# A conditioned hybrid decoder layer: the Pool-weight fold in four groups over blocks, the gate in the output-side stage, and own rings for two sets of small and large tiles

## The chip, the cores and the metric

The kernel runs on one core of one Trainium2 chip. Its time is the device time of one launch in microseconds (us), given as the median of several runs. One execution of the kernel before was also recorded by the hardware profiler; all rows that are quoted come from that execution. The engines are PE (matrix products; its weight loads are listed as PEld), DVE (vector), ACT (scalar functions), POOL and SP. SP issues nearly all transfers between main memory and the on-chip memory, in order.

## The reference

The layer works on x of 4096 tokens by 1024 channels, in float32, with one conditioning vector c.

```
shift, scale, gate = split(SiLU(c) @ w_ada + b_ada)          # 3 x 1024
h   = LN(x) * (1 + scale) + shift
u_a | z_a | glu_b | z_b = split(h @ w_in + b_in)             # 512, 512, 1024, 512
y_a = SiLU(z_a) * ls * (GroupLinear(CausalMultiPool(u_a) - u_a) + b_pool)
v   = glu_b[:, :512] * sigmoid(glu_b[:, 512:])
y_b = SiLU(z_b) * (SiLU(LN(DWConv31(v)) * g + b) @ w_pw + b_pw)
y   = concat(y_a, y_b) @ w_out + b_out
out = LN(2 ** 0.25 * x + gate * y) * ln_post_g + ln_post_b
```

CausalMultiPool is a trailing mean over 2, 4, 8 or 16 tokens, one width for each group of 128 channels. Pooling acts along the tokens and GroupLinear along the channels, so the weights of GroupLinear can be multiplied into the u_a part of w_in ahead of time. The kernel does this, and the document calls it the fold.

## The kernel before

**Tiling.** Tokens are cut in eight blocks (sb) of T = 512, each of TT = 4 row tiles of 128 tokens. Channels are cut in KT = 8 slices of 128 (k). Every float32 matrix is split in a high part in PE's reduced float32 type and the low rest (`split`, L194): ACT makes the high part with a copy, DVE subtracts it from the source. `mm3` (L336) makes one product of three matmuls: high times high (L337), high times low (L338), low times high (L339). A chunk is 128 output channels for one block: 8 slices of 3 matmuls of 512 columns, 24 in all.

**Stages.** Stage 1 (L461) goes over the eight blocks. In each it makes ten chunks: eight for the gated unit of mixer B (chunk pairs 8+m and 12+m, m = 0 to 3) and two of z_b (`z_half`, L454). Stage 2 (L512) reads the normalised x again from main memory (xD, written in stage 1) and makes ten more chunks a block: z_a, u_a and the rest of z_b. Between matmuls DVE runs the depthwise convolution of finished blocks (`conv`, L558), which takes most of its time, and `conv_ln` (L588) its LayerNorm. Stage 3 (L761) makes the second product of mixer B and the output product, with the last two blocks' convolutions beside it.

**The first block** is made in another way than the others. Its four x tiles are loaded by row (`load_x`, L258) and normalised (L375 to L377). `mod_block` (L173) works out shift and scale for one or two slices of channels: eight DVE steps multiply the w_ada tiles by SiLU(c) and add them up in `macc` (L179, L181), and PE sums `macc` over the partitions by a matmul with one column of ones (L186). `turn_x` (L313) transposes x on PE, and `mod_turned` (L319) applies scale and shift and makes the high and the low part (L321, L323, L324). The rows of w_in for the eight gated chunks (`load_row`, L389) are 128 by 1024 and are split by `split_cols` (L402), 768 and then 256 columns. Block 0 then runs six of its eight gated chunks k by k over six banks (L420), and the last pair, m = 3, in the loop at L473.

**The other blocks** of stage 1 are prepared one block ahead. `row_stats` (L278) loads four row tiles, takes their mean and variance by two ACT passes (`col_stats`, L263: L265 and L267) with small DVE steps and a power on POOL (L269), turns the results to rows (`to_rows`, L271), writes them out and reads them back to all partitions (`xbc`, L286). `norm_T` (L289) loads transposed x and applies the statistics on DVE (L292, L294); `mod_xT` (L298) adds the shift and makes the high part on ACT (L303) and the low part on DVE (L304), and stores both to xD (L306).

**The work that the change moves.** Behind block 0, `fold_u` (L350) is called four times, once for each group g: it loads a slice wT of the transposed w_in (L352), makes 16 matmuls of 128 columns (L358), two copies on ACT, a store, and one small matmul for the bias. Behind block 1, `mod_gate` (L140) adds up the gate from eight w_ada tiles on DVE, and four matmuls spread it over the partitions (L495). The 16 stores of block 0's xT (L439) stand behind the first block's products, with a wait for the last step of `mod_block`.

**Buffers.** A tag names a ring of buffers; a tile waits until the ring's oldest tile has been read. The tag `tm` (5 buffers) holds x tiles, `xbc` and `norm_T`'s tiles; `wraw` (2) holds raw weights; `gate` and `gbo` (1 each) hold weight rows, then the gate and the output bias; `ca` (6) holds w_ada tiles and then convolution tiles; `sm` (4) and `rows8` (2) are shared by the statistics of x and of the convolution.

**Order.** The program is written stage by stage, and a scheduler writes out the order on each engine from a simulated timeline; each engine then works strictly in that order. A few orders are given by hand with `after` (L84).

Of the kernel before, what the change touches and what calls it, by code (L numbers as in the profile page):

```python
# [9 lines left out]
F32 = mybir.dt.float32  # L10
# [7 lines left out]
P = 128  # L18
# [15 lines left out]
EARLY = 2  # L34
PERSB = (1, 1, 1, 1, 1, 1, 0, 0)
# [4 lines left out]
def tile_layer(ctx, tc, x, x_t, w_in_t, c, w_ada, b_ada, w_in, b_in, w_pool, b_pool, ls_pool, w_dw, b_dw,  # L40
# [132 lines left out]
    def mod_block(b, k0, nk, wts):  # L173
# [3 lines left out]
        for kt in range(KT):  # L177
# [6 lines left out]
        for i in range(2):  # L184
            for j in range(nk):
                nc.tensor.matmul(ps[:, nk * i + j : nk * i + j + 1], acc[:, 1 - i, j * P : (j + 1) * P],  # L186
                                 ones[:, 0:1], start=True, stop=True)
# [33 lines left out]
    def stats_dve(src, n, pre, i):  # L221
        nh = n // 512
        bs = st.tile([P, nh, 6], F32, tag=f"{pre}bs", bufs=4, name=f"{pre}bs{i}")
# [34 lines left out]
    def load_x(i):  # L258
        xt = ph.tile([P, D], F32, tag="tm", bufs=5, name=f"x{i}")
        nc.sync.dma_start(xt, tok(xv, i))  # L260
# [27 lines left out]

    def norm_T(sb, bc, k):  # L289
        z = ph.tile([P, 2, T], F32, tag="tm", bufs=5, name=f"xk{sb}_{k}")  # L290
        nc.sync.dma_start(z, x_t[k * P : (k + 2) * P, sb * T : (sb + 1) * T].rearrange("(k p) s -> p k s", p=P))
# [58 lines left out]
    def fold_u(g, wpl):  # L350
        wT = wraw(f"wT{g}")
        nc.sync.dma_start(wT, w_in_t[g * P : (g + 1) * P, :])  # L352
        wf = wraw(f"wf{g}")
        for hb in range(2):
            pb = s2_bank(f"fv{g}_{hb}")
# [6 lines left out]
        pb = s2_bank(f"bu{g}")  # L362
# [39 lines left out]
    def split_cols(k, m0, m1):  # L402
        split(*(t.rearrange("p (h c) -> p h c", h=2)[:, :, m0 * P : m1 * P] for t in (*Wg[k], rows[k])))
# [31 lines left out]
    gate_bc = cst.tile([P, D], F32, tag="gate", name="gate_bc")  # L435
    gbo = cst.tile([P, D], F32, tag="gbo", name="gbo")
    for k in range(KT):
        for i in range(2):
            after(nc.sync.dma_start(xD[k][0][:, i, :], xT[k][i].bitcast(F32)), last, True)  # L439

# [20 lines left out]
    for sb in range(NSB):  # L461
# [17 lines left out]
        if sb == 0:  # L479
# [6 lines left out]
            for g in range(MC):  # L486
                fold_u(g, wpl)
        if sb == 1:
            mod_gate(gbo)
            gb = wraw("gb")  # L490
            nc.sync.dma_start(gb, b_ada[2 * D : 3 * D].partition_broadcast(P))
            for h in range(2):
                sl = slice(h * 512, (h + 1) * 512)
                gp = tp_bank(f"gp{h}")
                nc.tensor.matmul(gp, ones, gbo[:, sl], start=True, stop=True)  # L495
                nc.vector.tensor_tensor(gate_bc[:, sl], gp, gb[:, sl], op=ALU.add)
            nc.sync.dma_start(gbo, b_out.partition_broadcast(P))
            nc.vector.tensor_tensor(gbo, gbo, gate_bc, op=ALU.mult)
# [3 lines left out]

    ph_ctx = ExitStack()
# [302 lines left out]
```

## Time and profile before

| | |
|---|---|
| median of 3 runs | 1403.74 us |
| the runs | 1396.62, 1403.74, 1404.29 us |
| the profiled execution | 1397.84 us |
| its span, first to last instruction | 1395.8 us |
| mean granted clock of PE | 0.992 |
| busy: PE, DVE, ACT, POOL | 1356.4, 1193.9, 432.6, 131.0 us |
| share of the span: PE, DVE, ACT, POOL | 97%, 86%, 31%, 9% |
| moved by DMA | 243.81 MB, mean 175 GB/s |

The span leaves out 2.0 us around the first and the last instruction. A row of the view by stretches gives, for a stretch of the span, the busy time and the number of instructions of each engine, the granted clock of PE, the busy share of the DMA engines and GB/s. A row of the timeline gives start, length, engine, line, operation, output and inputs, shapes and count, and in brackets the idle time of that engine just ahead and what ended it. A row of the chain gives start, length, and the engine and line, or the DMA, that the end waited for then.

### The profile page before, as it was taken

What the parts mean: (1) busy time and instruction counts of PE and PEld (TensorE: products, weight loads), DVE (VectorE), ACT (ScalarE), POOL (GpSimd) and SP (SyncE); (2) the same over time, 40 slices, a digit from 0 to 9 for tenths busy, and PEclk for the clock granted to TensorE, in tenths of its full rate; (3) what the DMA queues carried; (4) which work ended last, traced back from release to release, by engine and by line L of the source; (5) the groups of instructions that cost most, each with busy time, mean ns of one, the idle gap of its engine ahead of it and who ended that gap; (6) DMA issues with size and microseconds to landing.
All of it is one profiled execution on the core that took longest, in us unless ns stands there. A gap on an engine that the chain in (4) does not pass through costs nothing.

```text
span 1395.8 us, 17137 instructions
## 1 busy us (share of the span) xinstructions
PE 1356.4 (97%) x6045; PEld 1118.5 (80%) x6045; DVE 1193.9 (86%) x2348; ACT 432.6 (31%) x772; POOL 131.0 (9%) x193
## 2 busy tenths in 40 slices
PE   4898999999999999999999999999999999999997
PEld 3777888888888888888888888888888888888886
DVE  8688989983569999899899699999997899998754
ACT  3544235245531231411114111343234131322310
POOL 1000000010100001210111110100111101001111
PEclk9999999999999999999999999999999999999999
DMA  9958677477563662360541723466444443433511
GB/s 323 328 180 323 214 275 267 163 267 235 180 249 124 226 194 83 131 233 23 182 139 59 234 67 123 131 203 196 157 167 148 139 159 118 162 129 130 186 61 76
DMA packets 113352, 243.81 MB, mean 175 GB/s; under 512 B 15027, under 2 KB 45555, under 8 KB 113267
## 3 DMA queue, kind: packets, MB, share of 16 engines
q1 hardware_dynamic: 103984, 209.15, 43.4%
q0 software_dynamic: 9216, 33.56, 7.2%
q8 instruction: 47, 0.77, 0.2%
q14 instruction: 39, 0.31, 0.1%
q10 hardware_dynamic: 66, 0.02, 0.0%
HBM read 156.65 MB, written 86.04 MB: 174 GB/s over the span
## 4 chain that ended last, share of the span: by engine, by line
PE 90%; DMA 5%; DVE 2%; ACT 2%; SPq 1%; issue 1%; DVEq 0%; ACTq 0%
PE po L713 25%; PE p L338 6%; PE p L339 6%; PE p L337 6%; PE p2z L338 4%; PE p2u L338 4%; PE p2z L337 4%; PE p2z L339 4%; PE p2u L337 4%; PE p2u L339 4%; PE pw L689 2%; PE pw L691 2%; PE pw L690 2%; PE p2b L338 2%; PE p2b L337 2%; PE p2b L339 2%
## 5 line engine op out<-in xcount | busy, mean ns | idle before, releaser
L576 DVE SCALAR_TENSOR_TENSOR cx<-cv,wdw,cx 128x513 f32<-128x513 f32 (+1 forms) x240 | 145.7, 613 | 0.7
L576 DVE SCALAR_TENSOR_TENSOR ca<-cx,wsum,ca 128x256 f32<-128x256 f32 (+1 forms) x240 | 143.7, 611 | 0.1
L576 DVE SCALAR_TENSOR_TENSOR ca<-cv,wdw,ca 128x256 f32<-128x256 f32 (+1 forms) x224 | 134.3, 611 | 0.0
L742 POOL TENSOR_TENSOR ors<-ove,mhalf 128x1 f32<-128x1 f32 x32 | 46.9, 1467 | 408.8 <-DVE ove L738 400.4
L736 ACT ACTIVATE ojk<-r,osm 128x1024 bf16<-128x1024 f32 x31 | 35.6, 1148 | 148.3 <-DVE osm L733 148.3
L332 POOL DMA_DIRECT2D x2r<-xD x64 | 34.8, 544 | 402.8 <-PE p2b L339 276.7
L731 DVE SCALAR_TENSOR_TENSOR r<-po,r 128x512 f32<-128x512 f32 x62 | 40.9, 687 | 22.0 <-PE po L713 21.9
L576 DVE SCALAR_TENSOR_TENSOR lx<-lv,wdw,lx 128x257 f32<-128x257 f32 x120 | 57.5, 479 | 0.0
L576 DVE SCALAR_TENSOR_TENSOR la<-lx,wsum,la 128x256 f32<-128x256 f32 x120 | 57.3, 478 | 0.0
L576 DVE SCALAR_TENSOR_TENSOR la<-lv,wdw,la 128x256 f32<-128x256 f32 x112 | 53.3, 478 | 0.0
L269 POOL TENSOR_TENSOR xcs<-smx,mhalf 128x1 f32<-128x1 f32 x28 | 20.7, 740 | 343.9 <-DVE smx L268 343.6
L517 ACT ACTIVATE sz<-p2z,cols 128x512 f32<-128x512 f32 x32 | 22.0, 688 | 95.6 <-PE p2z L339 95.5
L292 DVE TENSOR_TENSOR xk<-xk,xbc 128x1024 f32<-128x1024 f32 x28 | 34.1, 1222 | 17.2 <-DMA xk<-in_x_t_dram 17.2
L303 ACT ACTIVATE x<-xk,shc 128x512 fp32r<-128x512 f32 x56 | 38.0, 719 | 31.5 <-DVE xk L294 31.5
L304 DVE SCALAR_TENSOR_TENSOR x<-xk,shc,x 128x512 fp32r<-128x512 f32 x56 | 40.4, 749 | 8.3 <-ACT x L303 8.3
L524 ACT ACTIVATE u<-p2u,bu 128x512 f32<-128x512 f32 x32 | 22.0, 689 | 70.4 <-PE p2u L339 70.4
L745 DVE SCALAR_TENSOR_TENSOR r<-r,ors,b_bc 128x1024 f32<-128x1024 f32 (+1 forms) x33 | 41.1, 1248 | 3.2 <-POOL ors L742 3.1
L443 ACT ACTIVATE sg<-p,cols 128x512 f32<-128x512 f32 x32 | 21.9, 686 | 70.3 <-PE p L339 69.8
L265 ACT ACTIVATE x<-x 128x1024 f32<-128x1024 f32 x28 | 29.6, 1059 | 40.6 <-DMA x<-in_x_dram 39.7
L713 PE MATMUL po<-wo0h,ya 128*128 128x512 f32 x128 | 41.2, 392 | 0.0
L713 PE MATMUL po<-wo1h,ya 128*128 128x512 f32 x128 | 41.1, 390 | 0.0
L705 DVE SCALAR_TENSOR_TENSOR r<-r,gbo 128x1024 f32<-128x1024 f32 x32 | 39.0, 1218 | 1.7 <-DMA r<-in_x_dram 1.7
(360 smaller groups left out, 4107.4 us busy)
## 6 DMA issues: line engine op xcount, KB each, us to landing
x2r<-xD POOLq DMA_DIRECT2D x64, 512.0 KB, 7.3
xD<-x SPq DMA_DIRECT2D x56, 512.0 KB, 5.4
x<-in_x_dram SPq DMA_DIRECT2D x32, 512.0 KB, 6.8
r<-in_x_dram SPq DMA_DIRECT2D x32, 512.0 KB, 3.6
out_dram<-r SPq DMA_DIRECT2D x31, 512.0 KB, 2.6
xk<-in_x_t_dram SPq DMA_DIRECT2D x28, 512.0 KB, 8.2
wa<-in_w_ada_dram SPq DMA_DIRECT2D x32, 256.0 KB, 6.4
vD<-v SPq DMA_DIRECT2D x32, 256.0 KB, 2.2
```

Source lines behind the costliest of these rows:

```text
L303: nc.scalar.activation(h2[:, 0, :], z, AF.Identity, bias=shc[:, k : k + 1])
L304: nc.vector.scalar_tensor_tensor(h2[:, 1, :], z, shc[:, k : k + 1], h2[:, 0, :].bitcast(F32), op0=ALU.add, op1=ALU.subtract)
L337: nc.tensor.matmul(ps, w[0], X[0], start=first, stop=False)
L338: nc.tensor.matmul(ps, w[0], X[1], start=False, stop=False)
L339: nc.tensor.matmul(ps, w[1], X[0], start=False, stop=last)
L576: nc.vector.scalar_tensor_tensor(dst, src, wt, dst, op0=ALU.mult, op1=ALU.add)
L705: xg = nc.vector.scalar_tensor_tensor(r, r, ALPHA, gbo, op0=ALU.mult, op1=ALU.add)
L713: mm = nc.tensor.matmul(po[h], lhs, Wo[k][wi][:, h * 512 : (h + 1) * 512], start=(k == 0 and wi == 0 and lhs is yh), stop=last)
L731: nc.vector.scalar_tensor_tensor(r[:, sl], po[h], 1.0, r[:, sl], op0=ALU.mult, op1=ALU.add, accum_out=sm[:, h : h + 1])
L736: nc.scalar.activation(jk, r, AF.Square, bias=sm[:, 2:3], accum_out=ss)
L742: nc.gpsimd.tensor_tensor(rs, ve, mhalf[:, 0:1], op=ALU.pow)
L745: nc.vector.scalar_tensor_tensor(r[:, sl], r[:, sl], rs, b_bc[:, sl], op0=ALU.mult, op1=ALU.add)
```

## The change

The fold goes from behind block 0 to blocks 2 to 5 of stage 1, one group in each, and each wT is issued one block ahead of its fold. Its banks are those of the transposes, and its result lies in the `tm` ring. The gate goes from behind block 1 of stage 1 to behind block 2 of stage 2 (`GATE_SB`). Until then the `gate` and `gbo` buffers hold weight rows, the raw z weights, and the x tiles behind the statistics of blocks 2 to 7; the four x tiles of block 1 lie in the `ca` ring and are issued ahead of block 0's products. The sum in `mod_block` takes six steps on DVE, and PE adds the last two slices by matmuls with one column of SiLU(c). Of a weight row only 768 columns are loaded and split ahead of block 0; the other 256 come behind block 0's six chunks. The 16 stores of xT stand behind the last `norm_T` load of block 1. `sm` and `rows8` become a ring each for x and for the convolution, and the ring of `bn_stats` results loses a buffer.

```diff
+GATE_SB = 2
...
-        for kt in range(KT):
+        nv = KT - 2
+        for kt in range(nv):
             if kt == 0:
                 nc.vector.tensor_scalar(acc, wts[kt], sc[:, 0:1], None, op0=ALU.mult)
...
-                nc.tensor.matmul(ps[:, nk * i + j : nk * i + j + 1], acc[:, 1 - i, j * P : (j + 1) * P],
-                                 ones[:, 0:1], start=True, stop=True)
+                o = ps[:, nk * i + j : nk * i + j + 1]
+                sl = slice(j * P, (j + 1) * P)
+                nc.tensor.matmul(o, acc[:, 1 - i, sl], ones[:, 0:1], start=True, stop=False)
+                for kt in range(nv, KT):
+                    nc.tensor.matmul(o, wts[kt][:, 1 - i, sl], sc[:, kt : kt + 1], start=False, stop=kt == KT - 1)
...
-    def load_x(i):
-        xt = ph.tile([P, D], F32, tag="tm", bufs=5, name=f"x{i}")
+    def load_x(i, home=None):
+        if home is None:
+            xt = ph.tile([P, D], F32, tag="tm", bufs=5, name=f"x{i}")
+        else:
+            xt = cst.tile([P, D], F32, tag=("gate", "gbo")[home], name=f"x{i}")
...
-        sm = st.tile([P, 3], F32, tag="sm", bufs=4, name=f"sm{name}")
+        sm = st.tile([P, 3], F32, tag=f"sm{name[0]}", bufs=4, name=f"sm{name}")
...
-        rows = st.tile([n, P], F32, tag="rows8", bufs=2, name=f"rows{name}", padded_shape=[4 * TT, P])
+        rows = st.tile([n, P], F32, tag=f"rows{name[0]}", bufs=1, name=f"rows{name}", padded_shape=[4 * TT, P])
...
-            xt = load_x(i)
+            xt = x_early[t] if sb == 1 else load_x(i, t % 2)
...
-    def fold_u(g, wpl):
-        wT = wraw(f"wT{g}")
-        nc.sync.dma_start(wT, w_in_t[g * P : (g + 1) * P, :])
-        wf = wraw(f"wf{g}")
+    def fold_u(g, wpl, wT):
+        wf = ph.tile([P, D], F32, tag="tm", bufs=5, name=f"wf{g}")
...
-            pb = s2_bank(f"fv{g}_{hb}")
+            pb = tp_bank(f"fv{g}_{hb}")
...
-        nc.sync.dma_start(rows[k], w_in[k * P : (k + 1) * P, 8 * P : 16 * P])
+        nc.sync.dma_start(rows[k], w_in[k * P : (k + 1) * P, 8 * P : 16 * P].rearrange(
+            "p (h c) -> p h c", h=2)[:, :, : 3 * P])
...
+    x_early = []
+    for t in range(TT):
+        xt = s2.tile([P, D], F32, tag="ca", bufs=6, name=f"x{TT + t}", padded_shape=[P, 2 * (HQ + T + 1)])
+        nc.sync.dma_start(xt, tok(xv, TT + t))
+        x_early.append(xt)
...
     for k in range(KT):
+        hi, lo = (both(t)[:, :, : 3 * P] for t in Wg[k])
+        nc.scalar.copy(hi, rows[k])
         xT.append(mod_turned(pb, k))
-        split_cols(k, 0, 3)
-        split_cols(k, 3, 4)
+        nc.vector.tensor_tensor(lo, rows[k], hi.bitcast(F32), op=ALU.subtract)
...
+    for q in range(2):
+        raw = wraw(f"w3r{q}").rearrange("p (k h c) -> p k h c", k=4, h=2)
+        for k in range(4):
+            nc.sync.dma_start(raw[:, k], both(w_in[(4 * q + k) * P : (4 * q + k + 1) * P, 8 * P : 16 * P])[:, :, 3 * P :])
+        for k in range(4):
+            hi, lo = (both(t)[:, :, 3 * P :] for t in Wg[4 * q + k])
+            split(hi, lo, raw[:, k])
...
-        raw = wraw(f"wzr{q}")
+        raw = cst.tile([P, D], F32, tag=("gate", "gbo")[q], name=f"wzr{q}")
...
-    for k in range(KT):
-        for i in range(2):
-            after(nc.sync.dma_start(xD[k][0][:, i, :], xT[k][i].bitcast(F32)), last, True)
...
         zs = norm_T(sb + 1, bc, 4) + norm_T(sb + 1, bc, 6)
+        if sb == 0:
+            for k in range(KT):
+                for i in range(2):
+                    after(nc.sync.dma_start(xD[k][0][:, i, :], xT[k][i].bitcast(F32)), x_loads[1])
         z_half(sb, xT)
...
-            for g in range(MC):
-                fold_u(g, wpl)
-        if sb == 1:
-            mod_gate(gbo)
...
+        if 1 <= sb <= MC:
+            wT = wraw(f"wT{sb - 1}")
+            nc.sync.dma_start(wT, w_in_t[(sb - 1) * P : sb * P, :])
+        if 2 <= sb <= MC + 1:
+            fold_u(sb - 2, wpl, wTs.pop(0))
+        if 1 <= sb <= MC:
+            wTs.append(wT)
...
             nc.sync.dma_start(zD[1][sb][:, m - 2, :], sz)
+        if sb == GATE_SB:
+            mod_gate(gbo)
...
```

More of the change, by code (lines that the diff above doesn't have):

```diff
@@ L222, in stats_dve @@
         nh = n // 512
-        bs = st.tile([P, nh, 6], F32, tag=f"{pre}bs", bufs=4, name=f"{pre}bs{i}")
+        bs = st.tile([P, nh, 6], F32, tag=f"{pre}bs", bufs=3, name=f"{pre}bs{i}")
         for h in range(nh):
@@ L287, in row_stats @@
         return bc
+    x_loads = {}
     def norm_T(sb, bc, k):
         z = ph.tile([P, 2, T], F32, tag="tm", bufs=5, name=f"xk{sb}_{k}")
-        nc.sync.dma_start(z, x_t[k * P : (k + 2) * P, sb * T : (sb + 1) * T].rearrange("(k p) s -> p k s", p=P))
+        x_loads[sb] = nc.sync.dma_start(z, x_t[k * P : (k + 2) * P, sb * T : (sb + 1) * T].rearrange("(k p) s -> p k s", p=P))
         nc.vector.tensor_tensor(z, z, bc[:, 0:1, :].to_broadcast([P, 2, T]), op=ALU.add)
@@ L348, in inproj @@
         return banks
-    def fold_u(g, wpl):
-        wT = wraw(f"wT{g}")
-        nc.sync.dma_start(wT, w_in_t[g * P : (g + 1) * P, :])
-        wf = wraw(f"wf{g}")
+    wTs = []
+    def fold_u(g, wpl, wT):
+        wf = ph.tile([P, D], F32, tag="tm", bufs=5, name=f"wf{g}")
         for hb in range(2):
-            pb = s2_bank(f"fv{g}_{hb}")
+            pb = tp_bank(f"fv{g}_{hb}")
             for j in range(4):
@@ L361, in fold_u @@
         nc.sync.dma_start(uD[g], wf)
-        pb = s2_bank(f"bu{g}")
+        pb = tp_bank(f"bu{g}")
         nc.tensor.matmul(pb[:, 0:1], wpl[:, g, :], vec("b_in", g), start=True, stop=True)
@@ L391, in load_row, with both @@
         rows[k] = (wraw(f"wr{k}") if home < 2 else
-                   cst.tile([P, D], F32, tag=("gate", "gbo")[home - 2], name=f"wr{k}"))
-        nc.sync.dma_start(rows[k], w_in[k * P : (k + 1) * P, 8 * P : 16 * P])
+                   cst.tile([P, D], F32, tag=("gate", "gbo")[home - 2], name=f"wr{k}"))[:, : 6 * P].rearrange(
+                       "p (h c) -> p h c", h=2)
+        nc.sync.dma_start(rows[k], w_in[k * P : (k + 1) * P, 8 * P : 16 * P].rearrange(
+            "p (h c) -> p h c", h=2)[:, :, : 3 * P])
+    def both(t):
+        return t.rearrange("p (h c) -> p h c", h=2)
     mods = ((0, 1), (1, 1), (2, 2), (4, 2), (6, 2))
@@ L400, in tile_layer @@
             load_row(k)
-    def split_cols(k, m0, m1):
-        split(*(t.rearrange("p (h c) -> p h c", h=2)[:, :, m0 * P : m1 * P] for t in (*Wg[k], rows[k])))
+    x_early = []
[3 more added lines that the diff above has]
+        x_early.append(xt)
     xT = []
@@ L434, in tile_layer @@
             W[16 + m].append((Wz[k // 4][0][:, a : a + P], Wz[k // 4][1][:, a : a + P]))
-    gate_bc = cst.tile([P, D], F32, tag="gate", name="gate_bc")
-    gbo = cst.tile([P, D], F32, tag="gbo", name="gbo")
-    for k in range(KT):
-        for i in range(2):
-            after(nc.sync.dma_start(xD[k][0][:, i, :], xT[k][i].bitcast(F32)), last, True)
     def glu(sb, m, pa, pg):
@@ L485, in tile_layer @@
             nc.vector.tensor_tensor(bpl, vec("b_pool", 0, 4), vec("ls", 0, 4), op=ALU.mult)
-            for g in range(MC):
-                fold_u(g, wpl)
-        if sb == 1:
-            mod_gate(gbo)
[L490 to L498, printed above, removed]
+        if 1 <= sb <= MC:
[5 more added lines that the diff above has]
+            wTs.append(wT)
     ph_ctx.close()
     lt = pool("lt", reuse_waits="tile")
+    gate_bc = cst.tile([P, D], F32, tag="gate", name="gate_bc")
+    gbo = cst.tile([P, D], F32, tag="gbo", name="gbo")
     ph_ctx = ExitStack()
@@ L554, in tile_layer @@
             nc.sync.dma_start(zD[1][sb][:, m - 2, :], sz)
+        if sb == GATE_SB:
+            mod_gate(gbo)
+            gb = wraw("gb")
+            nc.sync.dma_start(gb, b_ada[2 * D : 3 * D].partition_broadcast(P))
+            for h in range(2):
+                sl = slice(h * 512, (h + 1) * 512)
+                gp = tp_bank(f"gp{h}")
+                nc.tensor.matmul(gp, ones, gbo[:, sl], start=True, stop=True)
+                nc.vector.tensor_tensor(gate_bc[:, sl], gp, gb[:, sl], op=ALU.add)
+            nc.sync.dma_start(gbo, b_out.partition_broadcast(P))
+            nc.vector.tensor_tensor(gbo, gbo, gate_bc, op=ALU.mult)
     ph_ctx.close()
@@ L718, in out_tile @@
         if fin:
-            bs = st.tile([P, 2, 6], F32, tag="xbs", bufs=4, name="obs")
+            bs = st.tile([P, 2, 6], F32, tag="xbs", bufs=3, name="obs")
             for h, sl in enumerate(halves):
```

2 lines of the change are left out of this document (1 added, 1 removed).

## The prediction

> **What bounds the kernel now.** I read the span first, then the busy time of each engine stage by stage, then the waits of PE, and last the chain of work for the stage in which PE is not busy.
>
> ```profile
> span 1395.8 us, 17137 instructions
> ```
> ```profile
> 20.40:35.80 15.40, 13.14 (x49) 10.45 (x50) 15.18 (x30) 6.28 (x12) 0.00 (x0) 0.90 1.09 365
> 35.80:71.40 35.60, 31.56 (x154) 25.62 (x153) 20.62 (x46) 19.84 (x33) 1.10 (x2) 1.00 0.96 324
> 71.40:93.60 22.20, 22.20 (x100) 18.24 (x99) 19.40 (x48) 7.19 (x12) 1.62 (x2) 1.00 0.61 205
> 93.60:114.70 21.10, 14.33 (x64) 12.73 (x63) 20.82 (x39) 10.08 (x18) 0.00 (x0) 0.68 0.65 202
> 114.70:150.00 35.30, 35.30 (x169) 29.32 (x168) 30.35 (x81) 13.57 (x25) 2.89 (x4) 1.00 0.81 287
> 150.00:420.00 270.00, 269.39 (x1193) 221.06 (x1192) 201.00 (x362) 116.88 (x189) 17.29 (x24) 1.00 0.66 233
> 420.00:700.00 280.00, 280.00 (x1254) 231.73 (x1254) 264.31 (x437) 63.10 (x121) 26.84 (x44) 1.00 0.44 148
> 700.00:940.00 240.00, 240.00 (x1082) 198.66 (x1081) 223.85 (x498) 62.87 (x139) 25.74 (x40) 1.00 0.42 137
> 940.00:1390.00 450.00, 447.95 (x1984) 368.76 (x1982) 382.13 (x767) 124.34 (x219) 50.43 (x40) 1.00 0.40 142
> ```
>
> Columns: stretch, its length, busy time of PE, PE's weight loads, DVE, ACT and POOL, granted clock, DMA share, GB/s. From 114.7 us on PE has no idle time but 0.61 us before 420 and 2.05 us at the very end: there PE's work is the time, and nothing that the other engines do earlier or later is worth anything until it makes PE wait. What can be won lies before 114.7 us: 2.26 us of idle PE in the first row, 4.04 in the second, 6.77 in the fourth, and a clock of 0.68 there. At full clock one large matmul costs 43.57/192 = 0.227 us:
>
> ```profile
> 1012.90 43.57 PE po L713 x192
> ```
>
> The fourth row is the fold of the Pool weights behind block 0. The chain of waits there:
>
> ```profile
> 93.66 1.79 PE fv L358 x16
> 95.44 0.03 PE bu L363
> 95.48 4.35 DMA wT<-in_w_in_t_dram
> 99.83 0.14 issue
> 99.96 3.75 PE fv L358 x16
> 103.72 0.03 PE bu L363 x2
> 103.75 4.54 DMA wT<-in_w_in_t_dram
> 108.28 0.14 issue
> 108.42 3.76 PE fv L358 x16
> 112.18 0.43 PE p L338
> ...
> 113.88 0.85 PE p L337 x2
> ```
>
> A fold takes 1.79 us at full clock and 3.75 at half: twice PE waits for the next wT, whose load starts only when the two wraw buffers come free, and the waits bring the clock down, so that the ten block-1 matmuls up to 114.73 run at 0.43 us as well (four singles and two in the last rows, and four in this one):
>
> ```profile
> 97.62 2.07 PE L337 MATMUL p<-x,wg0h 128*128 128x512 f32 x4 [2.01 <-ACT x L303]
> ```
>
> **The change part by part.** *A: the fold leaves this place.* From 93.66 to 114.73 are 21.07 us. The work in them, at full clock, is 3 x 1.79 + 10 x 0.227 = 7.6 us, so 13.4 us are idle and half clock. That work stays and is done in blocks 2 to 5, where the clock is 1.00; each wT is issued a block (some 54 us, 240 x 0.227) ahead of its fold, against 4.35 us that it takes. The fold's copies on ACT and its two transpose banks lie beside work; cover gone, each fold pays a wait like the 4.4 us above. **A = -13.4 us, if block 1 is ready at once.** Is it? In the kernel before it is not:
>
> ```profile
> 49.06 7.12 SPq L439 DMA_DIRECT2D xD<-x  x11
> ```
> ```profile
> 62.67 0.82 SPq L260 DMA_DIRECT2D x<-in_x_dram  x2
> ```
> ```profile
> 75.94 0.55 POOL L269 TENSOR_TENSOR xcs<-smx,mhalf 128x1 f32<-128x1 f32 x1 [2.25 <-DVE smx L268]
> ```
> ```profile
> 90.26 1.23 DVE L292 TENSOR_TENSOR xk<-xk,xbc 128x1024 f32<-128x1024 f32 x1
> ```
> ```profile
> 103.93 0.76 DVE L304 SCALAR_TENSOR_TENSOR x<-xk,shc,x 128x512 fp32r<-128x512 f32 x1
> ```
> ```profile
> 113.45 0.75 DVE L304 SCALAR_TENSOR_TENSOR x<-xk,shc,x 128x512 fp32r<-128x512 f32 x1 [0.28 <-ACT x L303]
> ```
>
> The last two x tiles of block 1 are issued at 62.67, behind the stores of block 0's xT on SP's queue and behind the five tm buffers; so the statistics end at 76.5, the norm starts at 90.26, and the low halves are done from 104.7 to 114.2, with conv steps between. In the changed kernel the four tiles have buffers of their own and are issued right behind the weights, and the 16 stores go behind the last x_t load (they then stand ahead of block 2's x tiles, which have a block's time). Bytes ahead of the x tiles fall by 1 MB (the last quarter of each half of the weight rows comes later), which is 2.9 us at the 365 GB/s of the first row. I put the end of the statistics at 62, some 14 us earlier: first low half at 91, last at 100. PE ends block 0 at about 93 and needs the last k nine us later (8 x 6 x 0.227 = 10.9 for a pass of two chunks). Residual wait: between 0 and 10, I take **+1.0**.
>
> *B: block 0.* PE starts at 20.46 and is stopped three times:
>
> ```profile
> 20.46 0.79 PE L337 MATMUL p<-x,wg0h 128*128 128x512 f32 x1 [2.77 <-ACT wg0h L195]
> ```
> ```profile
> 32.02 1.30 PE L186 MATMUL mod<-ones,macc 128*128 128x1 f32 x8 [1.82 <-DVE macc L181]
> ```
> ```profile
> 50.17 1.66 PE L337 MATMUL p<-x,wg4h 128*128 128x512 f32 x6 [1.85 <-ACT x L321]
> 54.02 0.50 PE L338 MATMUL p<-x,wg4h 128*128 128x512 f32 x1 [2.18 <-DVE x L324]
> ```
> ```profile
> 57.04 0.79 PE mod L186 x8
> ```
> ```profile
> L181 DVE SCALAR_TENSOR_TENSOR macc<-wa,sc,macc x35: 474/743/753, 12.1 to 48.3; 128x512 f32<-128x512 f32 x21, 128x256 f32<-128x256 f32 x14
> L196 DVE TENSOR_TENSOR wg4l<-wr,wg4h x2: 421/690/960, 42.3 to 43.2; 128x768 fp32r<-128x768 f32 x1, 128x256 fp32r<-128x256 f32 x1
> ```
>
> The modulation gains 32 matmuls of one column on PE (16 outputs, two more each). Eight cost 1.30 us at half clock and 0.79 at full: 16 x 0.163 + 16 x 0.099 = +4.2, or 0 where PE would wait anyway; I take +4.2, as they sit in PE's queue ahead of block 0's matmuls. DVE loses ten macc steps (4 x 0.474 + 6 x 0.743 = 6.4 us) and, for later, eight low halves of 0.42 us (3.4). DVE is busy for 15.18 of 15.40 us in the first row, so this is on the path: the wait of 1.82 goes (-1.8), and what is late next is PE itself. The copy of a row's high half now stands ahead of the turned x on ACT, and the first matmul waits 2.77 us for that copy: between 0 and -2.8; the turned x itself comes hardly earlier, so I take -1.0. The waits of 1.85 and 2.18 come from one x tile of block 1 whose statistics stood in ACT's queue ahead of k = 4 before it had landed; they may go, or come fourfold (below): I take half, -2.0. The last quarter of the rows, now eight 128 KB loads and eight split pairs behind the six chunks, is needed at the fourth glu chunk and lies beside 33 us of PE work (144 x 0.227). **B = 4.2 - 1.8 - 1.0 - 2.0 = -0.6**, between -8.6 (4.2 hidden, all waits gone) and +16 (4.2, and 12.1 as in R2).
>
> *C: at nothing.* The gate's DVE steps (seven like the row below, near 12 us in all) go from block 1 of stage 1 to block 2 of stage 2; DVE is idle for 15.7 us of 420 to 700 and 16.2 of 700 to 940, which hides them; without that cover they push low-priority conv steps, at most 12 us, into a stage in which DVE is idle for 68 us. POOL's queue gets nothing. The rings of sm, rows and xbs change only which buffer is waited for; one wait of 0.61 us in 150 to 420 is the most they can win.
>
> ```profile
> L147 DVE SCALAR_TENSOR_TENSOR gbo<-wag,sc,gbo x7: 1272/1276/1281, 140.0 to 180.7; 128x1024 f32<-128x1024 f32 x7
> ```
>
> **Sum.** The profiled execution took 1397.84 us (span 1395.8, 2.0 around it): 1397.84 - 13.4 + 1.0 - 0.6 = 1384.8. The three runs are 1396.62, 1403.74 and 1404.29, so the profile is a run of the lower kind and 5.9 below the median. Nothing in the trace tells which kind the next runs are; I add half, 2.9: **1387.8 us**.
>
> **The rivals.** *R1, block 1 stays late.* If the conv steps still crowd out the norm, low halves end at 114.2 as now. By then PE has done some 45 block-1 matmuls instead of 10, 7.9 us more, but still owes three folds, 5.4: -2.5, so 1395.3, with the 2.9 above 1398.2. For it: DVE is busy 20.82 of 21.10 us in the fourth row. Against: the norm began the moment its inputs were there. *R2, four x tiles in ACT's queue.* One cost 1.85 + 2.18 = 4.0 us; four cost 12.1 more, and a return to half clock, which lasted from 108.42 to 114.73, 3.2. With B's credit of 2.0 lost: 1384.8 + 17.3 = 1402.1, with 2.9 1405. It cancels the gain once the third tile waits. Against: these loads now stand behind all weights.
>
> *R3, slower.* The x tiles of blocks 2 to 7 have two single buffers (gate and gbo) where a ring of five was. A tile keeps its buffer for the load and two passes:
>
> ```profile
> L265 ACT ACTIVATE x<-x 128x1024 f32<-128x1024 f32 x28 | 29.6, 1059 | 40.6 <-DMA x<-in_x_dram 39.7
> ```
> ```profile
> x<-in_x_dram SPq DMA_DIRECT2D x32, 512.0 KB, 6.8
> ```
>
> That is 6.8 + 2 x 1.06 and small steps, near 9.5 us, two rounds 19 to 24, and the norm comes behind. If the scheduler starts this a block late, PE waits in each of six blocks. A wait of 2.0 us and the half clock behind it (3.2, as above) are 31 us in all: 1384.8 + 31 = 1416, with 2.9 1419. It decides from 2.6 us in each block on. Against: 24 us of 54, and the buffers are free a block ahead. Here the Trainium skill speaks (TensorE: Matmul & The Clock Gate, "What's actually happening"): PE's clock falls to half only after an idle window of about 3.4 us. By that rule the six waits would cost 12 us and the case would come to 1399.7. The trace goes both ways: the waits of 1.85 and 2.18 us left the next mod matmuls at full speed (0.79 us for eight), the wait of 2.01 us at 97.62 was followed by half clock.
>
> *R4, PE warms up earlier.* PE starts at half clock and is still there at 32.02, where eight mod matmuls take 1.30 us and not 0.79. The stretch from 108.42 took 6.3 us of work to come back to full clock; without the stops the same 6.3 us from 20.46 end at 26.8. Full clock from there instead of from 33.3 (32.02 + 1.30) wins half of 6.5 us: 1381.5, with 2.9 1384.4. The same page and section puts warm-up at about 3.4 us of sustained work, which would give this time or a better one; the trace doesn't agree, since PE was still at half clock 12 us after its start.
>
> **How the numbers follow.** Forecast 0.62 (own range 1376 to 1396, by B's bounds and the 5.9 between runs), R4 0.12, R1 0.12, R2 0.08, R3 0.06. A measurement can tell about 0.5% here, 7.0 us: faster is below 1396.7, slower above 1410.8. Faster: 0.62 + 0.12 + a third of R1 = 0.78; same: the rest of R1 and R2 = 0.16; slower: R3 = 0.06. Range 1374 to 1400: it takes in R4 with the mod matmuls hidden, the forecast and R1, and leaves out R2, R3 and 0.04 at the ends.
>
> **What would show it.** A is right if no fold matmul waits for a DMA and the clock stays 1.00 from 60 us on; wrong if PE waits for DVE's L304 steps or ACT's L303 at the start of block 1 (R1). B is right if the waits of PE on macc go and the mod groups last near 2.4 us each for two columns; R2 would show as ACT waiting for x with hi copies behind it. R3 would show as PE waits at the start of blocks 2 to 7. C is wrong if PE waits on DVE near 940. The prediction fails if the order that the scheduler writes out differs from the one before in places that I take as kept.

## The result, and the profile after

The changed kernel takes 1391.07 us, median of 6 runs (1389.84 to 1391.82), against 1404.01 for the kernel before on the same chip (6 runs, 1396.62 to 1406.83). The ratio is 0.9916, with a 95% interval of 0.9892 to 0.994: faster by 0.8%. The forecast was 1387.8, range 1374 to 1400. The profiled executions took 1397.84 and 1391.32 us, so that by them the gain is 6.5 us and not 13. The kernel before has runs near 1395 and runs near 1405 (22 later ones: 1393.3 to 1398.8 and 1402.6 to 1407.7; of 21 others two lie between, near 1400; 8 others are all below 1397), which the experiments below do not explain, and its profile is of the shorter kind.

The first fence holds the span and the line of busy times from the page of the changed kernel.

```profile
span 1389.5 us, 17281 instructions
...
PE 1362.0 (98%) x6109; PEld 1125.1 (81%) x6109; DVE 1189.8 (86%) x2338; ACT 436.0 (31%) x774; POOL 132.1 (10%) x193
```

PE is busy for 5.6 us more than before (1356.4) in a span that is 6.3 us shorter: 11.9 us of idle time are gone, and half of it was filled with something. Next, the view by stretches of the changed kernel, with the stretches and columns of the prediction.

```profile
20.40:35.80 15.40, 15.40 (x74) 13.35 (x74) 14.17 (x28) 5.91 (x9) 0.00 (x0) 1.00 1.10 359
35.80:71.40 35.60, 35.60 (x178) 29.82 (x177) 19.34 (x47) 27.50 (x48) 3.27 (x6) 0.90 0.80 254
71.40:93.60 22.20, 21.32 (x96) 17.32 (x95) 12.53 (x32) 9.41 (x17) 1.77 (x4) 1.00 0.89 295
93.60:114.70 21.10, 18.01 (x73) 14.21 (x72) 21.10 (x43) 13.98 (x21) 0.53 (x1) 0.92 1.01 377
...
940.00:1382.00 442.00, 441.62 (x1954) 363.19 (x1952) 358.90 (x718) 117.00 (x208) 52.71 (x39) 1.00 0.39 136
```

PE's idle time in the fourth row falls from 6.77 to 3.09 us and its clock rises from 0.68 to 0.92; this was the aim of the argument. In the second row the 4.04 us of idle time are gone, but the clock is down to 0.90 where it was 1.00, without any idle time. The waits of PE in the changed kernel (who waited for whom, us in total, times, longest):

```profile
PE mod L190 <- DVE macc L183: 10.4, 2, 9.3
PE p L348 <- DVE x L314: 2.9, 1, 2.9
...
PE p L347 <- ACT sg L463: 0.9, 1, 0.9
```

The first one lies ahead of the first product. The second is new and tells that block 1 is still late: L314 is the low half of x, L304 of the kernel before.

To see where the time was won I take three points of the program: the first product of z_b in stage 1 (p1z, behind block 0's gated chunks), of stage 2 (p2z) and of stage 3 (pw). These are the groups by tile, first of the kernel before, then of the one after; behind the three durations (shortest, median, longest, ns) stand the first and the last start.

```profile
L337 PE MATMUL p1z<-x,wz0h x64: 387/389/396, 82.6 to 452.9; 128*128 128x512 f32 x64
...
L337 PE MATMUL p2z<-x2r,w4h x64: 389/389/476, 502.2 to 898.7; 128*128 128x512 f32 x64
...
L689 PE MATMUL pw<-vp,wpw0h x64: 388/396/483, 946.5 to 1345.5; 128*128 128x512 f32 x64
```

```profile
L347 PE MATMUL p1z<-x,wz0h x64: 389/389/395, 85.2 to 445.7; 128*128 128x512 f32 x64
...
L347 PE MATMUL p2z<-x2r,w4h x64: 389/389/793, 496.8 to 893.5; 128*128 128x512 f32 x64
...
L720 PE MATMUL pw<-vp,wpw0h x64: 388/393/478, 939.7 to 1339.2; 128*128 128x512 f32 x64
```

Block 0 is 2.6 us slower (82.6 to 85.2), the rest of stage 1 is 8.0 us faster (419.6 to 411.6), stage 2 is 1.4 us faster (444.3 to 442.9) and stage 3 to the end 0.5 us slower (449.3 to 449.8). All experiments are read at the same points:

| kernel | p1z | p2z | pw | span | median us |
|---|---|---|---|---|---|
| before | 82.6 | 502.2 | 946.5 | 1395.8 | 1404.01 |
| after | 85.2 | 496.8 | 939.7 | 1389.5 | 1391.07 |
| after, second time | 84.3 | 493.9 | 936.8 | 1386.5 | 1390.73 |
| fold alone on before | 82.0 | 504.9 | 949.6 | 1422.0 | 1423.01 |
| fold's result in the ring, on before | 81.4 | 508.4 | 952.7 | 1402.1 | 1413.32 |
| after, fold back | 84.3 | 492.7 | 935.6 | 1385.1 | 1387.19 |
| after, no early x tiles | 88.0 | 508.3 | 956.1 | 1405.8 | 1408.03 |
| after, statistics' rows earlier | 83.9 | 490.6 | 943.4 | 1392.9 | 1395.13 |
| after, no modulation step on PE | 82.5 | 492.3 | 935.2 | 1384.7 | 1388.62 |
| after, four modulation steps on PE | 96.6 | 513.8 | 956.6 | 1406.3 | 1410.61 |
| no step on PE, rows earlier | 81.9 | 488.4 | 945.0 | 1395.3 | 1394.69 |
| no step on PE, fold back | 84.2 | 493.3 | 936.1 | 1385.9 | 1387.35 |

### The profile page after: what moved, and what is told of

It reads as the page before. It is cut to its first block, busy times and chain, and to the rows that moved or that the text cites. A ratio compares the mean times of both kernels' runs of the same rounds, so it can differ in the third digit from the quotient of the medians.

```text
span 1389.5 us, 17281 instructions
## 1 busy us (share of the span) xinstructions
PE 1362.0 (98%) x6109; PEld 1125.1 (81%) x6109; DVE 1189.8 (86%) x2338; ACT 436.0 (31%) x774; POOL 132.1 (10%) x193
## 4 chain that ended last, share of the span: by engine, by line
PE 95%; DMA 2%; DVE 1%; SPq 1%; ACT 0%; issue 0%; DVEq 0%; ACTq 0%
PE po L744 25%; PE p L348 8%; PE p L347 8%; PE p L349 8%; PE p2u L349 4%; PE p2z L348 4%; PE p2z L349 4%; PE p2u L348 4%; PE p2u L347 4%; PE p2z L347 4%; PE pw L722 2%; PE pw L720 2%; PE pw L721 2%; PE p2b L347 2%; PE p2b L348 2%; PE p2b L349 2%
## 5 line engine op out<-in xcount | busy, mean ns | idle before, releaser
L607 DVE SCALAR_TENSOR_TENSOR cx<-cv,wdw,cx 128x257 f32<-128x257 f32 (+1 forms) x240 | 147.1, 621 | 0.3
L314 DVE SCALAR_TENSOR_TENSOR x<-xk,shc,x 128x512 fp32r<-128x512 f32 x56 | 41.2, 752 | 1.9 <-ACT x L313 1.8
L200 ACT CAST yb<-z 128x512 fp32r<-128x512 f32 x32 | 19.8, 619 | 70.4 <-DVE z L727 59.7
```

The source lines that it names most:

```text
L314: nc.vector.scalar_tensor_tensor(h2[:, 1, :], z, shc[:, k : k + 1], h2[:, 0, :].bitcast(F32), op0=ALU.add, op1=ALU.subtract)
L607: nc.vector.scalar_tensor_tensor(dst, src, wt, dst, op0=ALU.mult, op1=ALU.add)
```

## The experiments

Two questions were open. Did the gain come from the place of the fold, as the prediction's part A has it, or from something else that makes block 1 ready earlier? And what brought the clock down in block 0 while PE was never idle? In the diffs, lines are cut to what differs.

**The kernel after, a second time**, beside another set of runs of the kernel before.

> The changed kernel again, on the chip of the next runs, for a comparison in one session. Its runs lie within 1389.8 to 1391.8 us, those of the kernel before spread from 1393 to 1408 in two groups; if the chip matters, this one moves as a whole; expected 1390 to 1392.

1390.73 us (10 runs, 1388.34 to 1392.5) against 1400.0 for before (21 runs): ratio 0.9931 [0.9903, 0.9958]. The medians repeat within 0.4 us; the profiled span is 3.0 us shorter than the first time, so differences of 3 us between single profiles carry nothing by themselves. Part of the 3.0 us is PE's clock: PE waits for block 1 again, for 2.55 us and not 2.86, but this time no half clock follows. The fourth row of the view by stretches, here with a clock of 1.00 and not 0.92:

```profile
93.60:114.70 21.10, 18.55 (x82) 14.96 (x81) 21.10 (x46) 13.16 (x20) 1.25 (x2) 1.00 1.02 378
```

From p1z to p2z this execution takes 409.6 us, the first one 411.6. Where an experiment is compared with the first profile below, this second one is the measure of what such a comparison is worth.

**The fold alone.** In the kernel before only the fold is moved, in four groups to blocks 2 to 5, with its banks and its buffers as in the change.

```diff
-        wf = wraw(f"wf{g}")
+        wf = ph.tile([P, D], F32, tag="tm", bufs=5, name=f"wf{g}")
...
-            for g in range(MC):
-                fold_u(g, wpl)
...
+        if 1 <= sb <= MC:
+            wT = wraw(f"wT{sb - 1}")
+            nc.sync.dma_start(wT, w_in_t[(sb - 1) * P : sb * P, :])
+        if 2 <= sb <= MC + 1:
+            fold_u(sb - 2, wpl, wTs.pop(0))
```

> The kernel before with the fold in four groups over blocks 2 to 5 and nothing else of the change. Theory L (the fold covered a late block 1, so that moving it alone is worth little): block 1's low halves end near 114 as before, PE waits for them, and the time is 2 to 5 us under the kernel before. Rival F (the fold's waits and their half clock are nearly the whole gain): 9 to 13 us under it, as the whole change.

1423.01 us (6 runs, 1420.73 to 1424.7) against 1398.26 (22 runs): ratio 1.0166 [1.0132, 1.0201]. It is slower, and neither theory had said so. The waits of PE in this kernel:

```profile
PE po L718 <- ACT ya L195: 13.5, 1, 13.5
...
PE p L337 <- ACT x L303: 7.7, 1, 7.7
PE p L338 <- DVE x L304: 6.0, 1, 6.0
PE pw L694 <- DVE z L701: 3.9, 1, 3.9
```

The second and the third stand at the start of block 1. With the fold gone from there PE has nothing to do until block 1 is ready: it waits 13.7 us, and stage 2 begins 2.7 us later than in the kernel before (504.9 to 502.2), though the prediction had put 13.4 us of idle time and half clock there down to the fold. So the fold had covered a late block 1. (The low halves of block 1 also begin 4.2 us later here, at 108.1 us and not 103.9, so not all of the 13.7 us had been covered before.) The other 23 us are lost in stage 3 (472.4 us from pw to the end against 449.3), 17.4 of them in the first and the last row; that the order which the scheduler writes there came out worse is the likely reason, and was not tried.

**The fold's result in the ring.** The same question without a move: the fold stays behind block 0, but its result leaves the two `wraw` buffers, so that wT need not wait.

```diff
-        wf = wraw(f"wf{g}")
+        wf = ph.tile([P, D], F32, tag="tm", bufs=5, name=f"wf{g}")
```

> The kernel before with one edit: the fold's result in the ring of five (tm) and not in the two wraw buffers, so that the next wT can be loaded during a fold; place, banks and all else as before. Theory B (the fold lost time to its buffers): the waits of 4.4 and 4.5 us for wT go, and 4 to 9 us are won at the first matmul of stage 2 (502.2 before), if block 1 is not late. Rival L (block 1 is late until 104 to 114 us and PE waits for it instead): PE waits for DVE's or ACT's steps of block 1, and less than 3 us are won.

1413.32 us (5 runs, 1404.02 to 1414.67) against 1396.02 (8 runs): ratio 1.0103 [1.007, 1.0136]. The profiled one is among the shortest, 1404.05; the highest of the 8 runs of before is 1396.6. The timeline of PE in this kernel (columns as in the prediction):

```profile
92.32 1.95 PE L358 MATMUL fv<-wpl,wT 128*128 128x128 f32 x16
96.59 1.25 PE L337 MATMUL p<-x,wg0h 128*128 128x512 f32 x4 [2.33 <-ACT x L303]
103.33 0.79 PE L338 MATMUL p<-x,wg0h 128*128 128x512 f32 x1 [5.49 <-DVE x L304]
...
110.66 1.14 PE L358 MATMUL fv<-wpl,wT 128*128 128x128 f32 x8
```

No fold matmul waits for a transfer any more; the two waits for wT (4.8 us) turned into longer ones for block 1, whose low halves begin at 102.5 us, hardly earlier than the 103.9 of before. The wait for wT was not what held PE. Half clock follows from 103.33 on, and stage 2 begins at 508.4.

**The fold back behind block 0, in the changed kernel.** Everything else of the change stays.

```diff
-        if sb == 1:
+        if sb == 0:
             wpl = s2.tile(
...
-        if 2 <= sb <= MC + 1:
-            fold_u(sb - 2, wpl, wTs.pop(0))
...
+        if sb == 0:
+            for g in range(MC):
+                wT = wraw(f"wT{g}")
+                nc.sync.dma_start(wT, w_in_t[g * P : (g + 1) * P, :])
+                fold_u(g, wpl, wT)
```

> The changed kernel with the four folds behind block 0 again, each wT loaded there; the rest as changed. Theory A (the fold's waits for wT and the half clock are the gain, whatever block 1 does): 1400 to 1404. Rival L (the fold covers the wait for block 1, and with the result in another ring the two wraw buffers let the loads run ahead): PE waits less than 5 us at the folds, and the time is within 5 us of the changed kernel, 1391 to 1396.

1387.19 us (6 runs, 1386.79 to 1389.23) against 1400.0 for before: ratio 0.9906 [0.9872, 0.9941]. It is no slower than the changed kernel but 3.5 us faster (1390.73 beside the same runs of before, lowest 1388.34), less time than either theory gave. The timeline of PE:

```profile
95.22 1.95 PE L368 MATMUL fv<-wpl,wT 128*128 128x128 f32 x16
...
99.13 0.50 PE L348 MATMUL p<-x,wg0h 128*128 128x512 f32 x1 [1.27 <-DVE x L314]
...
103.94 1.14 PE L368 MATMUL fv<-wpl,wT 128*128 128x128 f32 x8
```

The first group of the fold fills most of the gap in which the changed kernel waits, the others go between block 1's products, and the clock stays at 1.00 from 95 to 150 us. So the place of the fold is not the gain. What is left of the change in stage 1 behind block 0 is the early x tiles, the stores of xT behind the last load, and the gate and the rings, which can have won little there: from 114.7 to 420 us PE was idle for 0.61 us in the kernel before. The next run takes the early tiles away.

**No early x tiles.** In the changed kernel the last x tile of block 1 is issued at 45.17 us, where the kernel before had issued two at 62.67:

```profile
45.17 0.43 SPq L420 DMA_DIRECT2D x<-in_x_dram  x1
```

Here the four tiles go into the two buffers that the later blocks use, and are loaded where those are.

```diff
-    x_early = []
-    for t in range(TT):
-        xt = s2.tile([P, D], F32, tag="ca", ...)
-        nc.sync.dma_start(xt, tok(xv, TT + t))
-        x_early.append(xt)
...
-            xt = x_early[t] if sb == 1 else load_x(i, t % 2)
+            xt = load_x(i, t % 2)
```

> The changed kernel with the four x tiles of block 1 in the two single buffers (gate and gbo) like those of the later blocks, so that they are loaded in two rounds behind the raw z weights; the rest as changed. Theory X (the early x tiles are what lets block 1 start without the fold in front of it): block 1 comes some 9 us later, PE waits 10 to 13 us and falls to half clock, and the time is 1400 to 1405. Rival P (the place of the transposition xcp behind block 0's six chunks sets it): 1391 to 1394.

1408.03 us (4 runs, 1407.65 to 1410.33) against 1396.02: ratio 1.0091 [1.0076, 1.0106], some 17 us more than the changed kernel and slower than before. The waits of PE:

```profile
PE p L348 <- DVE x L314: 4.7, 1, 4.7
PE p L347 <- ACT x L313: 4.5, 1, 4.5
```

The first low half comes at 109.6 us instead of 99.6, and stage 2 begins 11.5 us later (508.3 to 496.8). Without the early tiles the rest of the change loses. No run adds the early tiles alone to the kernel before, so that they are needed is shown, and that they suffice is not. (The edit also puts four tiles into two buffers, so it shows that the tiles need early homes of their own, not how the gain is shared between early loads and more buffers.)

**The statistics' rows earlier.** In the changed kernel the statistics of block 1 end at 58.8 us, earlier than the 62 of the forecast, but their next step comes 14 us later. The timeline of the changed kernel:

```profile
58.28 0.55 POOL L277 TENSOR_TENSOR xcs<-smx,mhalf 128x1 f32<-128x1 f32 x1 [5.96 <-DVE smx L276]
...
72.97 0.27 PE L74 MATMUL xcp<-ident,xcs 128*8 128x128 f32 x1
...
99.57 0.75 DVE L314 SCALAR_TENSOR_TENSOR x<-xk,shc,x 128x512 fp32r<-128x512 f32 x1
...
100.38 0.80 PE L348 MATMUL p<-x,wg0h 128*128 128x512 f32 x1 [2.86 <-DVE x L314]
```

The step is a transpose on PE (xcp), and it stands in PE's queue behind the six chunks of block 0. Here `row_stats(1)` is called ahead of the last `turn_x`.

```diff
+            if k + 1 == KT - 1:
+                bc1 = row_stats(1)
             pb = turn_x(xt_next, k + 1)
...
-            bc = row_stats(sb + 1)
+            bc = row_stats(sb + 1) if sb else bc1
```

> The changed kernel with the statistics of block 1 written ahead of the last turn of block 0's x, so that the transposition of its statistics (xcp) can take its bank and its place in PE's queue there and not behind all six chunks (72.97 us in the changed kernel, though the statistics are done at 58.7). Theory W (that place sets when block 1 is ready): xcp at 59 to 64, the norm starts some 9 us earlier, and the wait of 2.86 us at 100.38 with the half clock behind it goes: 1391.1 - 4.5 = about 1386.5. Rival C (conv steps between the norm steps on DVE set it): the wait stays within 1 us, and so does the time.

1395.13 us (12 runs, 1393.68 to 1396.55) against 1398.26: ratio 0.9962 [0.9939, 0.9986], 4 us slower than the changed kernel. The wait for block 1 is gone, and stage 2 begins 6.2 us earlier (490.6 to 496.8; 3.3 earlier than in the second profile of the changed kernel, 493.9), but stage 2 itself takes 9.9 us more (452.8 to 442.9). The waits of PE:

```profile
PE ccp L74 <- POOL ccs L277: 3.8, 1, 3.8
...
PE cl L74 <- DVE ca L619: 2.7, 1, 2.7
```

Both are in the LayerNorm of a convolution, hundreds of us later (at 842 and 763 us), and the clock is at 0.97 over the 50 us around each, some 1.5 us more each: an edit of one call in stage 1 changed the order there. The reading of stage 1 held, the sum did not.

**No modulation step on PE**, and **four of them.** The changed kernel adds two of eight steps on PE.

```diff
-        nv = KT - 2
+        nv = KT
...
-                nc.tensor.matmul(o, acc[:, 1 - i, sl], ones[:, 0:1], start=True, stop=False)
+                nc.tensor.matmul(o, acc[:, 1 - i, sl], ones[:, 0:1], start=True, stop=nv == KT)
```

> The changed kernel with all eight modulation steps on DVE again and one matmul for each output on PE; the rest as changed. Theory M (the one-column matmuls cost more than the DVE steps that they replace): in the changed kernel the mod groups of two slices last 2.6 us and not 0.8, and the clock falls to half behind two of them (0.50 at 46 to 48 and 60 to 62 us) although PE is busy; without them both falls go, and the time is 1391.1 - 3 (1.8 for each of three groups, 3.6 of half clock, less DVE waits that come back) = about 1386 to 1389. Rival D (DVE is the path in the first 45 us, as my prediction had it): PE waits for macc again and the time is 1393 to 1396.

```diff
-        nv = KT - 2
+        nv = KT - 4
```

> The changed kernel with four modulation steps on DVE and four on PE: 64 more one-column matmuls than in the kernel before instead of 32. Theory M: a mod group of two slices lasts 40 x 0.108 = 4.3 us, the clock falls to half behind each of them and for longer; the time rises by 4 to 8 us, to 1395 to 1399. Rival D: DVE loses ten more steps and the time falls by 1 to 3, to 1388 to 1390.

None on PE: 1388.62 us (8 runs, 1385.5 to 1391.37), ratio 0.991 [0.9879, 0.9941], about 2 us faster than the changed kernel, as theory M had it. Four: 1410.61 us (9 runs, 1408.43 to 1412.04), ratio 1.0081 [1.0051, 1.0111], some 20 us slower. The view by stretches of the kernel with four (PE's clock is the third number from the end):

```profile
50.00:60.00 10.00, 8.39 (x36) 6.79 (x35) 4.27 (x22) 9.59 (x22) 1.64 (x3) 0.83 0.92 277
60.00:71.40 11.40, 10.62 (x60) 9.84 (x61) 4.04 (x7) 3.51 (x5) 0.00 (x0) 0.81 0.19 65
71.40:80.00 8.60, 8.60 (x36) 6.93 (x36) 1.37 (x5) 6.09 (x11) 1.10 (x2) 0.86 0.48 178
```

With none the clock of all three stretches is 1.00. The direction is that of the theory that such matmuls lower the clock; the 20 us are more than twice its price: block 0 alone ends 11.4 us later (p1z at 96.6 instead of 85.2), and 5.6 us more are lost up to p2z, where PE waits for block 1 for 4.7 and 2.2 us and not 2.9.

**One-column matmuls by themselves.** Six times in stage 2, in PE's queue behind a large matmul, the changed kernel gets 40 matmuls of one column (the result is not used), or 38 matmuls of 512 columns that last as long.

```diff
+            with tc.high_priority():
+                pb = tp_bank(f"dm{sb}")
+                prev = LAST[0]
+                for j in range(40):
+                    mm = nc.tensor.matmul(pb[:, j : j + 1], ident, ones[:, 0:1], start=True, stop=True)
+                    after(mm, prev)
+                    prev = mm
```

```diff
+                for j in range(38):
+                    mm = nc.tensor.matmul(pb, W[4][0][0], xT[0][0], start=True, stop=True)
```

> The changed kernel with a group of 40 one-column matmuls without use behind each of blocks 1 to 6 of stage 2, where PE has no idle time and the clock is 1.00. Each group lasts 40 x 0.108 = 4.3 us. Theory M (one-column matmuls count as idle for the clock): the granted clock falls to 0.50 behind the groups, for some 3.4 us each, and the time grows by 6 x (4.3 + 1.7) = 36 us. Rival N (PE's busy time counts, and the falls in block 0 had another cause): the clock stays 1.00 and the time grows by 26 us.

> The control to the narrow groups: the changed kernel with 38 matmuls of 512 columns without use behind each of blocks 1 to 6 of stage 2, 38 x 0.227 = 8.6 us a group, the same as the 80 one-column instructions of a narrow group would last at full clock (80 x 0.108). Theory M: the clock stays 1.00 behind the groups and the time is 1391 + 6 x 8.6 = 1443, some 45 us less than with the narrow groups (1488). Rival N (any break in the kernel's own work does it): near 1488.

Narrow: 1488.32 us, one run; wide: 1440.86 us, one run. The view by stretches around one narrow group (timeline: from 680.47 to 694.75):

```profile
680.00:682.00 2.00, 2.00 (x19) 1.91 (x17) 1.84 (x5) 1.72 (x4) 1.40 (x3) 1.00 1.02 351
682.00:684.00 2.00, 2.00 (x18) 2.00 (x17) 1.65 (x6) 0.22 (x2) 0.73 (x1) 0.88 1.18 411
684.00:694.00 10.00, 10.00 (x49) 10.00 (x48) 1.41 (x3) 0.00 (x0) 0.00 (x0) 0.50 0.74 271
694.00:700.00 6.00, 6.00 (x17) 4.39 (x18) 0.91 (x3) 1.47 (x4) 0.55 (x1) 0.50 0.00 0
700.00:702.00 2.00, 2.00 (x8) 1.56 (x8) 0.00 (x0) 0.00 (x0) 0.00 (x0) 0.85 0.00 0
```

And the stretch of the same group in the wide kernel (timeline: from 667.43 to 677.20) and behind it:

```profile
666.00:706.00 40.00, 40.00 (x188) 32.10 (x187) 25.82 (x61) 13.03 (x33) 7.94 (x13) 1.00 0.53 179
```

PE is busy without a gap in both. In the narrow one the clock falls to half some 3 us behind the group's start and comes back 6 us behind its end; in the wide one it stays at 1.00. A narrow group of 80 instructions would take 8.6 us at the 0.108 us that one takes at full clock (2.60 us for 24 in block 0), and took 14.1. The expectation had counted 40 instructions and 36 us in all, where 97 came; each float32 matmul is two. With both set to the same length at full clock, the 47 us between the kernels are half clock: the mean clock is 0.964 over 1486.5 us in the narrow kernel and 0.996 over 1439.0 in the wide one, which makes 53.5 and 5.8 us lost. (The narrow groups have the identity as weights and the wide ones weights of the layer. This pair does not tell the width from the values, but the groups in block 0, whose weights are values of w_ada and its sums, are followed by half clock too, two of three.)

**Two edits together.** The step on DVE with the earlier rows, and the step on DVE with the fold back, each with the diffs above.

> The changed kernel with all eight modulation steps on DVE and with block 1's statistics ahead of the last turn: the edits of the first and third experiment together. If they add up in stage 1 (-4.5 us at the first matmul of stage 2 for the one, -6.2 for the other) stage 2 starts near 486 us instead of 496.8, and with stages 2 and 3 as in the changed kernel the time is 1380 to 1383. Rival S (what is won in stage 1 is given back where the scheduler writes another order, as the third experiment lost 10 us to waits on the convolution's LayerNorm in stage 2): stage 2 starts near 486 and the time is 1388 or more.

> The changed kernel with all eight modulation steps on DVE and with the four folds behind block 0 again. If both were losses inside the change (-2.5 us by medians for the first, -3.5 for the second) and add up: 1384 to 1386. Rival S (each wins through the same wait for block 1, so that the second adds nothing, or stage 2 gives it back by another order): 1387 to 1390.

With the earlier rows: 1394.69 us (10 runs, 1393.08 to 1404.18), ratio 0.9964 [0.9937, 0.999]. Stage 1 is the best of all (p2z at 488.4, 8.4 us ahead of the changed kernel, 5.5 of its second profile), and stage 2 gives 13.7 us back (456.6 to 442.9):

```profile
PE cl L74 <- DVE lv L599: 6.4, 1, 6.4
PE ccp L74 <- POOL ccs L277: 3.3, 2, 2.8
```

With the fold back: 1387.35 us (4 runs, 1386.05 to 1387.93), ratio 0.9937 [0.992, 0.9953]. The two gains of 2 and 3.5 us do not add, as rival S had it: without the added matmuls PE waits in block 0 again, for x (3.1 us), for the high parts of w_in (2.7) and for the low parts of x (2.2). The fastest version found is one of the two with the fold back, which can't be told apart: 1387.2 to 1387.4.

## Why the number was right and its main reason was not

**A is the step that failed.** The prediction read the 13.4 us of idle time and half clock behind block 0 as the cost of the fold that stands there, so that moving it away would win them. Moving it alone won nothing in stage 1 (+2.7 us), taking its wait for wT away lost 6.2 us there, and with the fold back in its old place the changed kernel is 3.5 us faster. The sign that was given for A being wrong came, too: PE waits for L314 at the start of block 1, and the clock does not stay at 1.00 from 60 us on. The chain of waits named wT because this wait ended last of two that ran side by side; the other, for block 1's x, was there all the time and was covered. What won was what the prediction had only asked about as a condition: block 1 ready earlier, its statistics at 58.8 us and not 76.5, its first low half at 99.6 and not 103.9. Without the early x tiles, which then share two buffers, the change is slower than the kernel before. That the stores of block 0's xT now stand behind the last load was not tried by itself, nor were the early tiles, so the share of each stays open.

**The residual wait** was put at +1.0 us within 0 to 10. It is 2.86 us of idle time, and the half clock behind it (windows of 2 us: 0.50 at 100 to 102, 0.68 at 102 to 104) costs some 1.5 more; in the second profile it is 2.55 us without half clock. The statistics did end by 62 us, but the prediction took it that the rest would follow at once, with the first low half at 91, and xcp stood 14 us in PE's queue. The kernel before had shown such a stay, of 4 us behind the statistics that ended at 76.5:

```profile
80.42 0.27 PE L73 MATMUL xcp<-ident,xcs 128*8 128x128 f32 x1
```

Together A and this term were -12.4; from p1z to p2z 8.0 us were won, 10.0 by the second profile. So the size of the two together came near, for another reason than the one given.

**B** was -0.6 and came out at +2.6 (p1z; +1.7 in the second profile). The wait of 1.82 us for macc went, as did those of 1.85 and 2.18 for the x tile, so R2 didn't come. Two sizes were off. The added matmuls were counted as 32 instructions, though the page counts 6109 against 6045 on PE, 64 more; at 0.108 us they are 6.9 us and not 4.2. (The sign that was given, groups near 2.4 us, had the right count: they last 2.6.) And half clock behind the groups, without idle time, was not priced at all; it came behind two of the three groups of two slices. The timeline of PE in the changed kernel, and the view by stretches:

```profile
43.74 0.58 PE L192 MATMUL mod<-sc,wa 128*128 128x1 f32 x4
44.19 0.64 PE L74 MATMUL xt<-ident,x 128*128 128x128 f32 x4
...
44.89 0.39 PE L348 MATMUL p<-x,wg3h 128*128 128x512 f32 x1
...
45.42 0.63 PE L347 MATMUL p<-x,wg3h 128*128 128x512 f32 x1
```

```profile
46.00:48.00 2.00, 2.00 (x7) 1.52 (x6) 0.78 (x3) 2.00 (x4) 0.00 (x0) 0.50 1.01 328
```

A group of 24 one-column instructions (41.59 to 44.19) has just ended; about 1 us later the large matmuls go from 0.39 to 0.63 us. The clock of 0.90 over 35.6 us is 3.6 us lost. The first product came 2.0 us later (22.41, not 20.46) instead of 1.0 earlier, since the modulation of the second slice now stands ahead of it. These terms (6.2 us of idle time gone; 2.0 later, 5.2 for the 48 instructions behind the first product, 2.0 more half clock) make +3.0 at the end of the six chunks, where +1.4 was measured (72.86 to 71.42); 1.6 us stay unexplained. The rest up to p1z is mostly a new wait of 0.9 us, for ACT's sg step behind the six chunks.

**C** held: PE waits for nothing near 940 us, and stages 2 and 3 change by -1.4 and +0.5 us. But the experiments show that this was in part luck and no property of edits to stage 1: three others lost 10 to 23 us in the same stages.

**The rivals.** R1 showed its sign, a wait for L314, once and for 2.86 us; it is what the fold moved alone does, at +2.7 us in stage 1 where R1 had -2.5. R3's waits at blocks 2 to 7 don't appear. R4 rested on a misread row: the timeline of the kernel before has

```profile
26.55 1.61 PE L339 MATMUL p<-x,wg0l 128*128 128x512 f32 x6
```

that is 0.27 us for each, so PE had warmed up by then, and the half clock at 32.02 was a second fall behind the wait of 1.82 us. So the prediction's reading that PE was still at half clock 12 us after its start does not stand.

**The number.** On the scale of the profiled execution the forecast was 1384.8 and the result 1391.32, 6.5 us more: A with its residual 4.4, B 3.2 and stages 2 and 3 -0.9 make 6.7. Nothing cancels among the terms; the 2.9 us added for the median brought the forecast to within 3.3 us of the median that came. That was luck: all 16 runs of the changed kernel lie between 1388.3 and 1392.5, and nothing in them answers to the 2.9. The second profile, 1388.34, would leave 3.5 us and not 6.5 to explain.

## What to carry to other kernels

Where an engine is idle behind a piece of work, ask what it would do next if that piece were gone: two waits that run side by side show as the one that ends last, and moving work away from a gap helps only if what follows is ready. Price work put on PE by what it does to the clock, not only by its own time: matmuls of one column filled idle time and slowed the large ones behind them. With an order that a scheduler writes out for the whole program, judge an edit at points between the stages first, and by the total last.

## What the runs showed of the hardware

A stretch of one-column float32 matmuls does not keep PE's clock up: PE and its weight loads were busy for 10.00 of 10.00 us, and the clock was 0.50. Here the Trainium skill (TensorE: Matmul & The Clock Gate, "What's actually happening") says that the gate follows how busy PE has been in windows of about 3.4 us. The trace agrees in part: over the six narrow groups the clock fell 2.5 to 5.0 us behind the start of the group and came back 2.9 to 6.3 us behind its end (read in windows of 0.5 us), which is about the size of such a window, but no fixed delay. What the profile calls busy is not what the gate counts.

The start is slower than the clock column tells. In the changed kernel the timeline and the view by stretches have

```profile
25.82 2.73 PE L348 MATMUL p<-x,wg0h 128*128 128x512 f32 x6
28.39 1.53 PE L349 MATMUL p<-x,wg0l 128*128 128x512 f32 x6
```

```profile
26.00:28.00 2.00, 2.00 (x6) 1.61 (x6) 1.97 (x5) 1.51 (x3) 0.00 (x0) 1.00 1.09 354
```

that is 0.45 us for each at a column of 1.00, and then 0.26. The time to full speed is not fixed: it came 6.0 us behind the first large matmul here (22.41 to 28.39), some 5.3 in the kernel before (20.46 to 25.74, from where four one-column instructions take 0.42 us), and 3.2 in the kernel without a modulation step on PE (20.15 to 23.30). Nor does a wait decide by its length alone whether half clock follows: it followed a wait of 2.01 us in the kernel before (at 97.62) and the 2.86 us for block 1 in one execution of the changed kernel, and not the 2.55 us at the same place in the other.
